# Hymba block on one core: the token division of keys and values moves to 272, and the weights of six kinds start at a different even column in every quarter

## The chip, the cores and the metric

The kernel runs on one core of a Trainium2 chip. The metric is the device time of one execution in microseconds. The engines are named as in the profile: PE multiplies matrices (PEld is its loading of stationary weights), DVE is VectorE, ACT ScalarE, POOL GpSimd, and SP issues most of the DMA transfers.

## The reference

512 tokens and 16 meta tokens in front of them, 528 in all, each 2048 wide, go through one layer. Everything that the change touches belongs to the input projection `P`:

```python
hn = _rmsnorm(h_res, norm_in_g[l])
P = hn @ w_in[l]                    # (528, 2048) @ (2048, 8320)
Pr, Pc = P[..., :RW_COLS], P[..., RW_COLS:]
prev = jnp.pad(Pr[:, :-1], ((0, 0), (1, 0), (0, 0)))
Pr = Pr + (prev - Pr) * mu_shift[l]
...
y = _rwkv7_recurrence(r, decay, k, v, kk, kk * a)   # over the tokens, one after the other
...
y_b = Bg * _causal_depthwise_conv(Cg * hc, conv_w[l]) * jax.nn.silu(g_c)
...
h_res = h_res + jnp.concatenate([y_a, y_b], axis=-1) @ w_out[l]
return _rmsnorm(h_res, norm_f_g)[:, N_META:]
```

The 8320 columns of `w_in` are 65 tiles of 128: eight each of r, k, v, g (group A), one of the two low-rank inputs (lora), and eight each of B, C, h, gc (group B).

## The kernel before

**The input projection.** The input is held transposed, 16 tiles of 128 channels by 528 tokens, as a rounded part `xh` and a remainder `xl`, each of shape 128 x 16 x 576 (576 is `LX`, the room for a channel tile, of which 528 columns are used). A weight tile of 128 output columns over all 2048 channels comes in four quarters of 128 x 512, each holding the stationary weights of four channel tiles. `split_w` (line 135) makes of each quarter a rounded part `hi` on ACT (line 138) and a remainder `lo` on DVE or POOL (line 139). Each product of the projection is three matmuls: hi with xh, hi with xl, lo with xh (line 326). All of them add up in PSUM over the 16 channel tiles.

**The token ranges.** [...] `FULL` serves k, v and lora, which need all 528 tokens; `TAIL` serves r, g, C and h, which need 514; `REAL` serves B and gc, which need 512 and are done in one piece:

```python
FULL = ((0, 256), (256, L))       # L = 528
TAIL = ((14, 272), (272, L))
REAL = ((META, L),)               # META = 16
```

For each quarter, `steps` (line 317) runs the first range over four channel tiles (twelve matmuls) and then the second range over the same four. A tile of k thus has 96 matmuls: 48 of 256 columns and 48 of 272. A tile of r has 48 of 258 and 48 of 256; a tile of B 48 of 512. Each range has its own PSUM tile, which `scaled` copies out on DVE, one operation for each range. `shift_full` and `shift_real` then mix each token with the one before it.

**The weight slots.** `hi` and `lo` lie in one slot of a pool of six, 1088 columns wide, and `parts_of` (line 128) puts them behind an offset of `SHIFT[kind]` columns:

```python
SHIFT = {"lora": 16, "k": 16, "v": 16, "r": 32, "C": 64, "h": 32, "B": 16, "g": 32, "gc": 16, "out": 40}
```

The slots are 1088 columns apart, a multiple of 64, and the rows of xh are 576 apart, also a multiple of 64. So for one kind and one range, every weight block and every moving block start at the same column modulo 64. `kind_of` gives the kind of a stream position.

**The order.** PE's order is written out by hand. `mains` goes through the list `plan`: lora, k, r, B of index 0 first, interleaved quarter by quarter while the input arrives (its first products stand on line 485), and then one tile after the other. Between these matmuls, `fill` puts the smaller products of the recurrence when a given amount of projection work has passed; a matmul of n columns counts 0.43 n ns there. `prefetch` requests weights from SP and splits them two or three half tiles ahead. DVE, ACT and POOL are ordered by a scheduler. After the projection, the output projection runs (lines 1236 and 1445), whose moving weights lie in the same slots with offset 40.

Of the kernel before, what the change touches and what calls it, by code (L numbers as in the profile page):

```python
# [23 lines left out]
L = SEQ + META  # L24
# [50 lines left out]


LX = 576
SHIFT = {"lora": 16, "k": 16, "v": 16, "r": 32, "C": 64, "h": 32, "B": 16, "g": 32, "gc": 16, "out": 40}


@with_exitstack
def hymba_kernel(ctx: ExitStack, tc: tile.TileContext, xt, xtok, front, w_in, w_out, pv, lup, cst, msk, gf, out):
# [27 lines left out]
    plan = [("lora", 0), ("k", 0), ("r", 0), ("B", 0), ("v", 0), ("k", 1), ("r", 1), ("v", 1), ("g", 0), ("g", 1)]  # L110
# [10 lines left out]
    N_IN = len(stream)  # L121
# [5 lines left out]

    def parts_of(kind, name):
        t = wp.tile([P, 2 * 512 + 64], F32R, tag="hl", name=name, bufs=6)
        o = SHIFT[kind]  # L130
        return t[:, o : o + 512], t[:, o + 512 : o + 1024]

    def kind_of(j):
        return "out" if j >= N_IN else plan[j % 4 if j < 8 else j // 2][0]

    def split_w(q, rq, eng):
        hi, lo = parts_of(kind_of(q // 2), f"w{q}")
        nc.scalar.copy(hi, rq)  # L138
        low[q] = eng.tensor_tensor(out=lo, in0=rq, in1=hi.bitcast(F32), op=ALU.subtract).ins  # L139
        quarters[q] = (hi, lo)  # L140
# [36 lines left out]
    def tm(name):  # L177
        return tp.tile([P, LP], F32, tag="tm", name=name, bufs=3)
# [52 lines left out]
    for n in range(4):  # L231
        quarters[2 * n] = parts_of(kind_of(n), f"w{2 * n}")
    F0, F1, F2 = KT + P + L, 4 * P + L, 8 * P + 2 * L
    fr = [view("bt", F0), view("r0", 3 * P), view("bk", F1), view("gt0", F2)]
    o = 0
# [61 lines left out]
    with tc.issue_after(head):  # L297
        nc.vector.tensor_scalar(
            out=omm, in0=pvt[:, V_MU : V_MU + 33], scalar1=-1.0, scalar2=1.0, op0=ALU.mult, op1=ALU.add
        )  # L300
        for d, off in (
# [4 lines left out]
                out=d, in0=pvt[:, off : off + 8], scalar1=0.5, scalar2=None, op0=ALU.mult  # L306
            )
        nc.vector.tensor_scalar(
            out=hv[:, 4], in0=pvt[:, V_KA : V_KA + 8], scalar1=-0.5, scalar2=1.0, op0=ALU.mult, op1=ALU.add
        )  # L310

    nc.scalar.copy(ones, cs[:, C_BM : C_BM + P + 2])
    FULL = ((0, 256), (256, L))
    TAIL = ((14, 272), (272, L))
    REAL = ((META, L),)

# [14 lines left out]
    def banks(ranges, name, pool, tag):  # L331
        return [pool.tile([P, b - a], F32, tag=tag, name=f"ps_{name}_{r}") for r, (a, b) in enumerate(ranges)]

    def main(j, ranges, name):
        prefetch(2 * j + 4)
        ps = banks(ranges, name, pm, "main")
        for k4 in range(4):
            if k4 == 1:
                prefetch(2 * j + 5)
            yield from steps(ps, ranges, k4, 4 * j + k4)  # L340
        return ps

    def scaled(ranges, ps, dst, base):
        for (a, b), p in zip(ranges, ps):
            nc.vector.tensor_tensor(out=dst[:, a - base : b - base], in0=p, in1=rs[:, a:b], op=ALU.mult)

    def shift_full(ps, m, name, dst):
        pr = tp.tile([P, L + 1], F32, tag="pr", name=f"pr_{name}", bufs=2)
        nc.gpsimd.memset(pr[:, 0:1], 0.0)
        scaled(FULL, ps, pr, -1)  # L350
        sh = tm(f"sh_{name}")[:, 0:L]
# [121 lines left out]
    def mains():  # L473
        pa = banks(FULL, "lora", pm, "main")
        pb = banks(FULL, "k0", pz, "tz")
        pc = banks(TAIL, "r0", pm, "main")
        pd = [pi.tile([P, SEQ], F32, tag="ser", name="ps_B0")]
        four = ((pa, FULL), (pb, FULL), (pc, TAIL), (pd, REAL))
        for k in range(4):
            for n, (ps, rg) in enumerate(four):  # L480
                if k == n == 0:
                    hi, lo = quarters[0]
                    for ww, xx, first in ((hi, xh, True), (lo, xh, False), (hi, xl, False)):
                        for p, (a, b) in zip(ps, rg):
                            nc.tensor.matmul(p, ww[:, 0:P], xx[:, 0, a:b], start=first, stop=False)
                            yield (b - a) * 0.43
                    continue
                yield from steps(ps, rg, 0, 2 * n, (k,))
        for k4 in range(1, 4):
            for n, (ps, rg) in enumerate(four):  # L490
                h = 4 * (k4 // 2) + n
                if k4 == 2:
                    prefetch(h + 3)
                if (k4, n) == (3, 3):
                    for ks, part in ((range(1), 0), (range(1, 3), 4), (range(3, 4), None)):
                        yield from steps(ps, rg, k4, 2 * h + k4 % 2, ks)
                        if part is not None:
                            token_scale(yb, part)
                        if part == 4:
                            use("lora", 0, pa)  # L500
                            use("k", 0, pb)
                    continue
                for r in range(2 if n < 3 else 1):
                    if (k4, n, r) == (3, 1, 1):
                        yb = token_scale_sums()
                    yield from steps(ps, rg, k4, 2 * h + k4 % 2, range(4), (r,))
        use("r", 0, pc)
        use("B", 0, pd)
        for j in range(4, len(plan)):
            what, i = plan[j]  # L510
            rg = FULL if what in ("k", "v") else REAL if what in ("B", "gc") else TAIL
            ps = yield from main(j, rg, f"{what}{i}")
            if (what, i) == ("h", 0):
                state["conv"] = low[4 * j + 6]
            if what == "gc" and i < 4:
                state["split"] = low[4 * j + 4]
            use(what, i, ps)
# [646 lines left out]
    U = {unit: u for u, unit in enumerate(units)}  # L1164
# [34 lines left out]
    def split_unit(unit, t, home=None):  # L1199
        for q in range(2):  # L1200
            rq = t()[:, q * 512 : (q + 1) * 512]
            if home is None:
                hi, lo = parts_of("out", f"o{U[unit]}_{q}")
            else:
                hi, lo = home[q]
            nc.scalar.copy(hi, rq)
            last = nc.vector.tensor_tensor(out=lo, in0=rq, in1=hi.bitcast(F32), op=ALU.subtract)  # L1207
            right[unit, q] = (hi, lo)
        if unit[:2] == (1, "M3"):
            last_low[unit[2]] = last.ins  # L1210

    def here(t, n):
        return xa[t][:, n * 512 : (n + 1) * 512] if n < 2 else xb[n - 2][:, t]
# [83 lines left out]
    def split_home(g):  # L1297
        f = ("S1", "S3", "S4", "S5")[g]
        tiles = [
            pw.tile([P, 4, HT], F32R, tag=f"{f}0{a}", name=f"home{g}{a}").rearrange("p a b -> p (a b)") for a in range(2)  # L1300
        ]
        split_unit(
            (1, "M2", g), passing(1, 1, 0, g),
            [(tiles[0][:, 512 * q : 512 * q + 512], tiles[1][:, 512 * q : 512 * q + 512]) for q in range(2)],
        )
# [7 lines left out]
    for half in range(2):  # L1313
        o = 28 * half
        for g in range(4):
            b = o + 4 + 4 * g
            if half == 0:
                if g == 3:
                    at(-1, begin_chain, 0, g)
                    at(0, split_unit, (0, "M1", g), chained(g))  # L1320
            else:
                at(o + g - 4, begin_chain, 1, g)
                at(o + g - 2, split_unit, (1, "M1", g), chained(g))
            at(max(o + g, b - 5), add_by_transfer, half, 0, 1, g)
            at(b - (6 if g else 5), request, half, 0, 1, g)
            at(b - (4 if g else 5), request, half, 1, 1, g)
            at(b - 2, split_unit, (half, "P5", g), chained(g))
            at(b - 1, add, passing(half, 0, 1, g), half, 1, 1, g)
            at(b - 1, split_unit, (half, "M7", g), passing(half, 0, 1, g))
            at(b, split_unit, (half, "M3", g), passing(half, 1, 1, g))  # L1330
            at(b, add, chained(g), half, 1, 1, g)
            at(b + 1, split_unit, (half, "Q6", g), chained(g))
            at(b + 2, add_by_transfer, half, 1, 0, g)
            at(U[half, "P4", g] - 2, split_unit, (half, "P4", g), chained(g))
            if half == 0:
                at(U[half, "M2", g] - 4, request, 0, 1, 0, g)
                at(U[half, "M2", g] - 2, split_unit, (0, "M2", g), passing(0, 1, 0, g))
            else:
                at(o + 13 + 2 * g, request, 1, 1, 0, g)
# [28 lines left out]
    for u, unit in enumerate(units):  # L1368
        half, prod, g = unit
# [53 lines left out]
    with tc.manual_schedule(engines={mybir.EngineType.DVE, mybir.EngineType.Activation, mybir.EngineType.Pool}):  # L1423
# [16 lines left out]
        for part in range(2):  # L1440
            cols = slice(256 * part, 256 * part + 256)
            for jj in range(8):
                hi, lo = right[(1, "M2", jj // 2), jj % 2]
# [4 lines left out]
            h = here(1, 2)[:, cols]  # L1448
# [70 lines left out]
```

## Time and profile before

| what | value |
|---|---|
| median of the runs | 1004.92 us (2 runs, 1004.75 and 1005.09) |
| span of the profiled execution, first to last instruction | 1003.4 us |
| busy time of PE, DVE, ACT, POOL | 992.7, 681.1, 394.9, 272.1 us |
| granted TensorE clock, mean | 0.998 |
| traffic with HBM | 136.92 MB read, 36.35 MB written |

No time of the profiled execution is given beside its span; the median of the runs is 1.5 us longer than that span. In the lists, a matmul or load is a group `line engine op out<-in` with shapes, count, busy time and the mean time of one record. `128*128 128x256` is a stationary block of 128 x 128 and a moving one of 256 columns. Matmuls overlap, so a record is longer than the distance from one start to the next. The chain that ended last gives the pieces of work in order of time, with start, length and count.

### The profile page before, as it was taken

The page shows a single profiled execution, that of the slowest core. Times are in us where ns is not written, and L with a number is a line of the kernel's source. Part 1 is how long each engine was busy: PE and PEld are TensorE (multiplying, and loading weights), DVE is VectorE, ACT ScalarE, POOL GpSimd, SP SyncE. Part 2 cuts the span into 40 slices and gives each one's busy share as a digit, 9 for nine tenths or more (in the row PEclk, how much of TensorE's full clock was granted, in tenths as well). Part 3 has the DMA queues.
Part 4 walks back from the last instruction along what each step waited for, and adds up shares of the span by engine and source line. Part 5 has one row for each costly group of instructions (what it writes and reads, how often), then busy time and mean ns, then how long its engine had stood idle before and what let it go on. Part 6 is the DMA issues. An engine that isn't in the chain of part 4 may idle for free.

```text
span 1003.4 us, 23673 instructions
## 1 busy us (share of the span) xinstructions
PE 992.7 (99%) x9723; PEld 914.6 (91%) x9723; DVE 681.1 (68%) x1247; ACT 394.9 (39%) x729; POOL 272.1 (27%) x284
## 2 busy tenths in 40 slices
PE   9999999999999999999999999999999999999996
PEld 8999999999998999998999998989889898788885
DVE  6777866587765569655569654245554597997897
ACT  7553423344323434323434322223232435546453
POOL 0122524233232323232423223223332333001001
PEclk9999999999999999999999999999999999999999
DMA  9525485546665364864263855968674688797654
GB/s 322 153 90 148 122 222 147 163 122 148 162 167 170 102 166 94 221 163 119 85 171 98 219 148 162 324 204 247 201 228 93 178 267 211 187 299 191 159 127 168
DMA packets 185036, 174.82 MB, mean 174 GB/s; under 512 B 121568, under 2 KB 142816, under 8 KB 184416
## 3 DMA queue, kind: packets, MB, share of 16 engines
q1 hardware_dynamic: 182336, 164.40, 57.0%
q0 software_dynamic: 2304, 8.39, 4.9%
q8 instruction: 76, 1.25, 0.5%
q10 hardware_dynamic: 288, 0.52, 0.1%
q14 instruction: 32, 0.26, 0.1%
HBM read 136.92 MB, written 36.35 MB: 173 GB/s over the span
## 4 chain that ended last, share of the span: by engine, by line
PE 91%; DVE 5%; issue 1%; DMA 1%; ACT 0%; POOL 0%; DVEq 0%; SPq 0%; ACTq 0%; POOLq 0%
PE ps_h L326 9%; PE ps_k L326 9%; PE ps_v L326 9%; PE ps_g L326 9%; PE ps_C L326 9%; PE ps_r L326 9%; PE ps_B L326 9%; PE ps_gc L326 9%; PE M L1236 5%; PE P L1236 2%; PE g L674 2%; DVE o L1207 2%; PE Q L1236 1%; PE ps_lora L326 1%; PE zs L999 1%
## 5 line engine op out<-in xcount | busy, mean ns | idle before, releaser
L139 POOL TENSOR_TENSOR w<-wr,w 128x512 fp32r<-128x512 f32 x119 | 172.2, 1447 | 360.9 <-ACT w L138 305.1
L138 ACT CAST w<-wr 128x512 fp32r<-128x512 f32 x252 | 153.2, 618 | 289.0 <-PE ps_C L326 48.7
L139 DVE TENSOR_TENSOR w<-wr,w 128x512 fp32r<-128x512 f32 x133 | 98.5, 746 | 104.4 <-ACT w L138 104.0
L326 PE MATMUL ps_k<-xh,w 128*128 128x256 f32 (+1 forms) x512 | 96.1, 285 | 0.0
L326 PE MATMUL ps_r<-xh,w 128*128 128x258 f32 (+1 forms) x512 | 95.1, 281 | 0.0
L326 PE MATMUL ps_v<-xh,w 128*128 128x272 f32 (+1 forms) x512 | 94.9, 284 | 0.0
L326 PE MATMUL ps_h<-xh,w 128*128 128x256 f32 (+1 forms) x512 | 94.6, 283 | 0.0
L326 PE MATMUL ps_C<-xh,w 128*128 128x256 f32 (+1 forms) x512 | 93.2, 281 | 0.0
L326 PE MATMUL ps_g<-xh,w 128*128 128x256 f32 (+1 forms) x512 | 92.1, 281 | 0.0
L326 PE MATMUL ps_B<-xh,w 128*128 128x512 f32 x256 | 83.5, 395 | 0.0
L326 PE MATMUL ps_gc<-xh,w 128*128 128x512 f32 x256 | 81.6, 393 | 0.0
L326 PEld LDWEIGHTS ps_k<-xh,w 128*128 128x128 f32 x512 | 80.4, 190 | 0.5
L326 PEld LDWEIGHTS ps_h<-xh,w 128*128 128x128 f32 x512 | 79.6, 188 | 1.3 <-issue 0.6
L326 PEld LDWEIGHTS ps_r<-xh,w 128*128 128x128 f32 x512 | 80.1, 188 | 0.3
L326 PEld LDWEIGHTS ps_v<-xh,w 128*128 128x128 f32 x512 | 79.9, 189 | 0.3
L326 PEld LDWEIGHTS ps_C<-xh,w 128*128 128x128 f32 x512 | 79.2, 188 | 0.6
L326 PEld LDWEIGHTS ps_g<-xh,w 128*128 128x128 f32 x512 | 79.1, 189 | 0.3
L326 PE MATMUL ps_k<-xl,w 128*128 128x256 f32 (+1 forms) x256 | 72.8, 284 | 0.0
L326 PE MATMUL ps_v<-xl,w 128*128 128x256 f32 (+1 forms) x256 | 72.6, 284 | 0.0
L326 PE MATMUL ps_h<-xl,w 128*128 128x258 f32 (+1 forms) x256 | 71.9, 281 | 0.5 <-issue 0.5
L326 PE MATMUL ps_g<-xl,w 128*128 128x258 f32 (+1 forms) x256 | 72.3, 282 | 0.0
L326 PE MATMUL ps_r<-xl,w 128*128 128x258 f32 (+1 forms) x256 | 72.0, 281 | 0.0
(321 smaller groups left out, 2258.9 us busy)
## 6 DMA issues: line engine op xcount, KB each, us to landing
wr<-in_w_in_dram SPq DMA_DIRECT2D x126, 512.0 KB
ct<-opd SPq DMA_DIRECT2D x64, 288.0 KB
wo<-in_w_out_dram SPq DMA_DIRECT2D x24, 512.0 KB
x<-in_w_out_dram POOLq DMA_DIRECT2D x16, 512.0 KB, 6.0
opd<-ar SPq DMA_DIRECT2D x8, 576.0 KB
opd<-gt SPq DMA_DIRECT2D x16, 288.0 KB
opd<-bt SPq DMA_DIRECT2D x64, 64.0 KB
x<-in_w_out_dram SPq DMA_DIRECT2D x8, 512.0 KB
```

What stands on the lines that cost most here:

```text
L138: nc.scalar.copy(hi, rq)
L139: low[q] = eng.tensor_tensor(out=lo, in0=rq, in1=hi.bitcast(F32), op=ALU.subtract).ins
L326: nc.tensor.matmul(ps[r], ww[:, w], xx[:, kt, a:b], start=(kt == 0 and n == 0), stop=(kt == KT - 1 and n == 2))
L674: nc.tensor.matmul(z[h][:, c - c0], bk[hs, c, h : h + 2, :].rearrange("p a s -> p (a s)"), ar[hs, c].rearrange("p a s -> p (a s)"), start= ...
L999: nc.tensor.matmul(d[hs, j], w, x[hs], start=(a == 0), stop=(a == b - 1))
L1207: last = nc.vector.tensor_tensor(out=lo, in0=rq, in1=hi.bitcast(F32), op=ALU.subtract)
L1236: nc.tensor.matmul(bank[s], left(prod, jj, m, s), w, start=(jj == 0 and n == 0), stop=(jj == 7 and n == 2))
```

## The change

Keys, values and lora are divided at token 272 in place of 256, so their two ranges have 272 and 256 columns in place of 256 and 272. The offset of a quarter in its slot depends on the kind, the tile's index `i` and the quarter's number `part` (0 to 3): for k, r and h it is 8 i + 2 part, for v, g and C 62 minus that. Over the eight tiles of a kind, each even number from 0 to 62 occurs once. lora, B and gc keep 16 and the output projection keeps 40.

```diff
-SHIFT = {"lora": 16, "k": 16, "v": 16, "r": 32, "C": 64, "h": 32, "B": 16, "g": 32, "gc": 16, "out": 40}
+OUT_SHIFT = 40
+
+
+def shift_of(what, i, part):
+    if what == "out":
+        return OUT_SHIFT
+    if what in ("B", "gc", "lora"):
+        return 16
+    n = 8 * i + 2 * part
+    return n if what in ("k", "r", "h") else 62 - n
...
     def parts_of(kind, name):
         t = wp.tile([P, 2 * 512 + 64], F32R, tag="hl", name=name, bufs=6)
-        o = SHIFT[kind]
+        o = shift_of(*kind)
         return t[:, o : o + 512], t[:, o + 512 : o + 1024]
...
     def kind_of(j):
-        return "out" if j >= N_IN else plan[j % 4 if j < 8 else j // 2][0]
+        if j >= N_IN:
+            return "out", 0, 0
+        return plan[j % 4] + (j // 4 * 2,) if j < 8 else plan[j // 2] + (j % 2 * 2,)
 
     def split_w(q, rq, eng):
-        hi, lo = parts_of(kind_of(q // 2), f"w{q}")
+        what, i, half = kind_of(q // 2)
+        hi, lo = parts_of((what, i, half + q % 2), f"w{q}")
...
-    FULL = ((0, 256), (256, L))
+    FULL = ((0, 272), (272, L))
```

More of the change, by code (lines that the diff above doesn't have):

```diff
@@ L1202, in split_unit @@
             if home is None:
-                hi, lo = parts_of("out", f"o{U[unit]}_{q}")
+                hi, lo = parts_of(("out", 0, 0), f"o{U[unit]}_{q}")
             else:
```

## The prediction

> **What bounds the kernel now.** I read the page's first two parts, then the waits of PE, then the chain that ended last.
>
> ```profile
> span 1003.4 us, 23673 instructions
> ...
> PE 992.7 (99%) x9723; PEld 914.6 (91%) x9723; DVE 681.1 (68%) x1247; ACT 394.9 (39%) x729; POOL 272.1 (27%) x284
> ...
> PEclk9999999999999999999999999999999999999999
> ```
>
> ```profile
> PE pwarm L187 <- DVE cold L184: 1.4, 1, 1.4
> PE ps_h L326 <- issue: 0.5, 1, 0.5
> PE M L1236 <- DVE o L1207: 0.5, 1, 0.5
> PE ps_lora L326 <- DVE xl L208: 0.2, 1, 0.2
> ```
>
> PE is busy for 99% of the span at a full granted clock, and its four waits sum to 2.6 us. So the time is the sum of the distances between PE's products, and an edit counts only as far as it changes such a distance. The runs' median, 1004.92 us, lies 1.5 us above the span of 1003.4; I carry these 1.5 us along.
>
> The chain shows whole output tiles of the input projection that no other work interrupts (start, length, count of products).
>
> ```profile
> 154.81 10.90 PE ps_gc L326 x48
> ...
> 282.54 11.31 PE ps_h L326 x96
> ...
> 421.11 11.20 PE ps_C L326 x96
> ...
> 469.87 11.57 PE ps_k L326 x96
> ...
> 532.78 11.54 PE ps_v L326 x96
> ...
> 619.32 11.38 PE ps_C L326 x96
> ```
>
> A gc tile is one range of 512 columns: 10.90/48 = 227.1 ns a product, 0.4435 ns a column. The other kinds take two narrow products where gc takes one. At gc's rate a pair of 272 and 256 columns would take 528 x 0.4435 = 234.2 ns; k takes 11.57/48 = 241.0 and v 240.4, so 6.5 ns more. A pair of 258 and 256 would take 228.0; C takes 233.3, later 237.1, and h 235.6: 5.3, 9.1 and 7.6 more, 7.3 in the mean. These excesses are what an address can change. The two C rows have the same widths and the same start columns, so addresses alone do not fix the distance: what stood before on PE matters too.
>
> The timeline shows both shares of a pair. Only every third product reads xl, so two of its rows span three products (start, length).
>
> ```profile
> 421.43 0.28 PE L326 MATMUL ps_C<-xl,w 128*128 128x258 f32 x1
> ...
> 421.79 0.28 PE L326 MATMUL ps_C<-xl,w 128*128 128x258 f32 x1
> ...
> 422.84 0.28 PE L326 MATMUL ps_C<-xl,w 128*128 128x256 f32 x1
> ...
> 423.18 0.28 PE L326 MATMUL ps_C<-xl,w 128*128 128x256 f32 x1
> ```
>
> ```profile
> 471.62 0.29 PE L326 MATMUL ps_k<-xl,w 128*128 128x272 f32 x1
> ...
> 471.99 0.28 PE L326 MATMUL ps_k<-xl,w 128*128 128x272 f32 x1
> ```
>
> So C's 258 columns take 0.36/3 = 120 ns and its 256 take 113, which is gc's rate; k's 272 take 123, which leaves 118 of k's 241 to its 256. The groups by shape say the same over the whole run; the second number behind the bar is the mean record, and of it I use differences alone, since a record also holds a constant tail.
>
> ```profile
> L326 PE MATMUL ps_k<-xh,w 128*128 128x272 f32 x256 | 53.4, 287 | 0.0
> ...
> L326 PE MATMUL ps_C<-xh,w 128*128 128x258 f32 x256 | 52.2, 284 | 0.0
> ...
> L326 PE MATMUL ps_h<-xh,w 128*128 128x256 f32 x256 | 51.7, 282 | 0.0
> L326 PE MATMUL ps_k<-xh,w 128*128 128x256 f32 x256 | 51.6, 283 | 0.0
> L326 PE MATMUL ps_r<-xh,w 128*128 128x256 f32 x256 | 51.1, 279 | 0.0
> L326 PE MATMUL ps_v<-xh,w 128*128 128x256 f32 x256 | 50.6, 281 | 0.0
> ...
> L326 PE MATMUL ps_g<-xh,w 128*128 128x256 f32 x256 | 49.9, 279 | 0.0
> L326 PE MATMUL ps_C<-xh,w 128*128 128x256 f32 x256 | 49.7, 278 | 0.0
> ...
> L1445 PE MATMUL end<-home,m 128*128 128x256 f32 x48 | 5.9, 283 | 0.0
> ...
> L1445 PEld LDWEIGHTS end<-home,m 128*128 128x128 f32 x48 | 5.9, 192 | 0.1
> ```
>
> ```profile
> L326 PEld LDWEIGHTS ps_k<-xh,w 128*128 128x128 f32 x512 | 80.4, 190 | 0.5
> ...
> L326 PEld LDWEIGHTS ps_h<-xh,w 128*128 128x128 f32 x512 | 79.6, 188 | 1.3 <-issue 0.6
> ...
> L326 PEld LDWEIGHTS ps_C<-xh,w 128*128 128x128 f32 x512 | 79.2, 188 | 0.6
> ```
>
> One width, 256, has means from 278 to 283: a band of 5 ns. Of the weight loads (PEld, the second fence), those of L1445 and of k, both with products of 283, are the longest, 192 and 190 ns; C's are 188.
>
> **The change, part by part.** It adds and removes no product, load, copy or transfer. There are 48 tiles of the six kinds with 96 narrow products each, 4608, and lora adds 96. Every count below is of these.
>
> *Division at 272.* The second range of k, v and lora becomes tokens 272 to 527, the moving columns that r, g, C and h have as their second range already, so a row of before shows this product. The means are 283 and 281 for k and v, and 279, 278, 279 and 282 for r, C, g and h: 282.0 against 279.5. If only the moving start counted, this gave 2.5 ns x (16 x 48 + 48 = 816) = 2.0 us. The range of 272 columns now begins at column 0 in place of 256; both are multiples of 64, and I put it at nothing.
>
> *Start columns of the weights.* Before, all offsets of these kinds are 16, 32 or 64, multiples of 16 columns. Afterwards each kind goes once through every even offset from 0 to 62 in its 32 quarters: 28 of 32 are no multiple of 16, and 16 of 32 no multiple of 4. No row of the input projection shows such a start. The bounds from the nearest rows:
> - Below: nothing streams faster than gc's columns. If every excess went, FULL pairs would give 6.5 x 816 = 5.3 us and TAIL pairs 7.3 x 32 x 48 = 11.2 us, in all 16.5.
> - Above: every product at the dear end of the band. The TAIL kinds' 256 go from 279.5 to 283, 3.5 x 1536 = 5.4 us; FULL's from 282 to 283, 0.8 us; the 1536 of 258 and the 816 of 272 columns have no dearer row, so I let them lose the whole band, 5 x 2352 = 11.8 us. In all +18.0.
>
> I take the middle of the band, 280.5, for products that are thrown over all starts: the row nearest to an unknown mixture is neither C's nor L1445's. That is +1.0 x 1536 = +1.5 us for the TAIL kinds' 256, and 280.5 - 282 = -1.5 x 816 = -1.2 us for FULL's, which already holds what is left of the 2.0 us above. For 258 and 272 I take +2 of the possible 5, +4.7 us, because they stand above gc's rate already (120 against 114, 123 against 121) and so may be partly in the bad state now. Sum of both edits: +5.0 us.
>
> [...]
>
> *The start.* lora's first range needs 272 columns of xh in place of 256, and xh's first tile is written in two halves of 264.
>
> ```profile
> 4.04 0.92 ACT L207 ACTIVATE xh<-in_bt 128x264 fp32r<-128x264 f32 x2
> ...
> 4.61 1.50 PE L485 MATMUL ps_lora<-xh,w 128*128 128x256 f32 x4
> ...
> 9.22 0.39 PE L326 MATMUL ps_lora<-xl,w 128*128 128x256 f32 x1 [0.23 <-DVE xl L208]
> ```
>
> PE's first product now waits for the second half, 4.96 in place of some 4.5 us: at most 0.4 us later. Half of this is covered by the 0.23 us that PE waits at 9.22 for VectorE's xl, which comes no later. I add 0.2 us; without cover it is 0.4.
>
> *Splits and evacuations.* The copies and subtractions write to other columns.
>
> ```profile
> L139 POOL TENSOR_TENSOR w<-wr,w 128x512 fp32r<-128x512 f32 x119 | 172.2, 1447 | 360.9 <-ACT w L138 305.1
> L138 ACT CAST w<-wr 128x512 fp32r<-128x512 f32 x252 | 153.2, 618 | 289.0 <-PE ps_C L326 48.7
> ```
>
> ACT waits for PE to free slots (48.7 us behind C alone), so the splits run ahead. A quarter lasts PE about 11.2/4 = 2.8 us, the six slots hold over 16 us, and a split is 0.62 + 1.45 us. Even a doubled POOL part would be hidden; without this cover it would be 1.45 us x 119. The evacuations keep their number. Some DMA issues on SP and a few DVE, ACT and POOL steps change places with a neighbour, behind the same cover. I put all this at nothing.
>
> **Sum:** 1003.4 + 5.0 + 0.2 + 1.5 = 1010.1 us.
>
> **The rivals.**
> *No effect of the weights' start* (0.22). Loads are hidden under products, and only the division counts: 1003.4 - 2.0 + 0.2 + 1.5 = 1003.1, with 1000 to 1005 about it. For it: the C tile at equal addresses differs by 11.38 - 11.20 = 0.18 us, as much as kinds with different offsets do. Against: k, with offset 16, has load records of 190 ns and dear 256s, C 188 and cheap ones.
> [...]
>
> *The varied starts break up the dear state* (0.17). A pair of C went from 233.3 to 237.1 ns and stayed there for a whole tile. If a constant start keeps such a state alive, changing it every quarter would end it. The floor is 1003.4 - 16.5 + 1.5 = 988.4; half of it is 997.
>
> *The load becomes the limit* (0.15), the slower side. Under 113 to 123 ns of product a load has little room: the dearest 256s, k's and L1445's, have the longest ones (against it: h, with 282 ns and loads of 188). If starts off the multiples of 16 lengthen a load by some ns, each narrow product grows by the same, while gc and B hide it under 227. At 5 ns, the band's width, on all 4608 this is 23.0 us: 1003.4 + 23.0 + 1.5 = 1027.9. It passes 2% (20.1 us) from 4.4 ns on all, or 8.7 ns on the half that are no multiples of 4.
>
> That the change does nothing to the program is excluded by the offsets in the diff.
>
> **How the numbers follow.** The forecast, 1006 to 1021, has 0.46. The likeliest time is 1010. The range 994 to 1027 leaves out the lower part of the second rival (0.07) and the upper part of the third (0.10). A change under 2% is about what a measurement of this kernel cannot tell for sure: 2% below is 984.8, under every floor above, so 0.01; 2% above is 1025, reached by most of the third rival, 0.12; between, 0.87.
>
> **What would show it.** In the groups by shape, k's and v's 256 should fall from 283 and 281 to about 280 or 281, those of r, g and C rise by about 1 ns, and 258 and 272 by about 2. In the chain, whole tiles of C above 11.2 us and of k near 11.6. B and gc must keep 10.90. If the means of all narrow shapes stand, the first rival is right; if PEld's records grow by as much as the products, the third. The prediction is wrong if PE gets waits beyond 2.6 us, or if B's and gc's products change.

## The result, and the profile after

The changed kernel takes 1010.9 us (median of 2 runs, 1010.77 to 1011.04) against 1004.92: a ratio of 1.0056, with a 95% interval of 1.004 to 1.0073. Its profiled execution has a span of 1008.8 us, 5.4 more than before.

From the page (the PE and clock rows) and from the list of PE's waits (who waited for whom, sum, times, longest):

```profile
span 1008.8 us, 23672 instructions
...
PE 998.1 (99%) x9723; PEld 919.3 (91%) x9723; DVE 675.7 (67%) x1247; ACT 394.1 (39%) x729; POOL 264.6 (26%) x284
...
PEclk9999999999999999999999999999999999999999
```

```profile
PE pwarm L200 <- DVE cold L197: 1.4, 1, 1.4
PE M L1249 <- DVE o L1220: 0.5, 1, 0.5
PE ps_h L339 <- issue: 0.4, 1, 0.4
PE ps_lora L339 <- DVE xl L221: 0.2, 1, 0.2
```

PE's busy time grew by 5.4 us, as the span did. Its waits sum to 2.5 us (2.6 before), and no DMA or split has moved onto the path. So the loss lies in the distances between products. The chain shows it tile by tile (start, length, count):

```profile
132.46 11.44 PE ps_C L339 x96
143.91 11.42 PE ps_h L339 x96
155.32 10.93 PE ps_gc L339 x48
...
385.67 11.64 PE ps_v L339 x96
...
472.97 11.71 PE ps_k L339 x96
...
802.36 11.38 PE ps_C L339 x96
```

C's first tile went from 11.20 to 11.44 us, h from 11.31 to 11.42, k from 11.57 to 11.71, v from 11.54 to 11.64; the late C tile stands at 11.38, and gc within 0.03. The groups by shape tell which half of a pair it was (mean record behind the second comma):

```profile
L339 PE MATMUL ps_k<-xh,w 128*128 128x272 f32 x256 | 54.2, 288 | 0.0
...
L339 PE MATMUL ps_h<-xh,w 128*128 128x256 f32 x256 | 52.9, 285 | 0.4 <-issue 0.4
L339 PE MATMUL ps_C<-xh,w 128*128 128x258 f32 x256 | 52.1, 284 | 0.0
...
L339 PE MATMUL ps_r<-xh,w 128*128 128x256 f32 x256 | 51.5, 281 | 0.0
...
L339 PE MATMUL ps_k<-xh,w 128*128 128x256 f32 x256 | 51.3, 281 | 0.0
L339 PE MATMUL ps_g<-xh,w 128*128 128x256 f32 x256 | 51.1, 281 | 0.0
L339 PE MATMUL ps_v<-xh,w 128*128 128x256 f32 x256 | 51.0, 280 | 0.0
L339 PE MATMUL ps_C<-xh,w 128*128 128x256 f32 x256 | 50.9, 282 | 0.0
```

The 256 of r, g, C and h rose by 2 to 4 ns, the 272 of k by 1, the 258 of C not at all. Summed over every distance from one start to the next in the two traces, the 5.4 us are: 256 of r, g, C, h +4.3; their 258 -0.9; 272 of k and v +2.0; 256 of k and v -0.2; lora and all the rest +0.3 (the parts are rounded).

### The profile page after: what moved, and what is told of

It reads as the page before. It is cut to its first block, busy times and chain, and to the rows that moved or that the text cites. A ratio compares the mean times of both kernels' runs of the same rounds, so it can differ in the third digit from the quotient of the medians.

```text
span 1008.8 us, 23672 instructions
## 1 busy us (share of the span) xinstructions
PE 998.1 (99%) x9723; PEld 919.3 (91%) x9723; DVE 675.7 (67%) x1247; ACT 394.1 (39%) x729; POOL 264.6 (26%) x284
## 4 chain that ended last, share of the span: by engine, by line
PE 93%; DVE 3%; DMA 1%; issue 1%; ACT 0%; SPq 0%; DVEq 0%; POOL 0%; ACTq 0%
PE ps_v L339 9%; PE ps_k L339 9%; PE ps_h L339 9%; PE ps_g L339 9%; PE ps_r L339 9%; PE ps_B L339 9%; PE ps_gc L339 9%; PE ps_C L339 8%; PE M L1249 5%; PE P L1249 4%; PE g L687 2%; PE Q L1249 2%; DVE o L1220 1%; PE ps_lora L339 1%; PE zs L1012 1%; PE zy L1016 1%
## 5 line engine op out<-in xcount | busy, mean ns | idle before, releaser
L152 POOL TENSOR_TENSOR w<-wr,w 128x512 fp32r<-128x512 f32 x119 | 164.4, 1383 | 381.7 <-ACT w L151 330.9
L152 DVE TENSOR_TENSOR w<-wr,w 128x512 fp32r<-128x512 f32 x133 | 95.4, 723 | 114.0 <-ACT w L151 103.8
L339 PE MATMUL ps_k<-xh,w 128*128 128x272 f32 (+1 forms) x512 | 96.5, 285 | 0.0
L339 PE MATMUL ps_v<-xh,w 128*128 128x256 f32 (+1 forms) x512 | 96.4, 285 | 0.0
L339 PE MATMUL ps_k<-xl,w 128*128 128x272 f32 (+1 forms) x256 | 73.0, 285 | 0.0
L339 PE MATMUL ps_v<-xl,w 128*128 128x272 f32 (+1 forms) x256 | 72.8, 284 | 0.0
```

What stands on the lines that cost most here:

```text
L339: nc.tensor.matmul(ps[r], ww[:, w], xx[:, kt, a:b], start=(kt == 0 and n == 0), stop=(kt == KT - 1 and n == 2))
```

## The experiments

Each kernel is the kernel before with the edit shown. Ratios are to runs of the kernel before on the same chip, with their 95% interval. "Distance" below is the start column of a product's weights in their slot less the start column of its tokens in the row of xh, modulo 64. The two areas are taken to begin at the same place modulo 64 columns. The traces do not show this; if it were otherwise, every distance would be off by one constant, and no comparison below would change.

### The two edits alone

```diff
-    FULL = ((0, 256), (256, L))
+    FULL = ((0, 272), (272, L))
```

> Only the division of keys, values and lora at token 272; all offsets of the weights as before. If the moving start decides, as the prediction took it, the 256 columns of k and v fall by about 2.5 ns each and the 272 stand: 2.0 us less than before, 1002.9. Rival: at offset 16 the 272 keep their 123.5 ns and the 256 go to about 119.4, which is what the few quarters with offset 16 show in the changed kernel; then it is 1.4 us more than before, 1006.3. If the division alone were the cause of the whole loss it would be 1010.9.

1007.17 us, ratio 1.0021 (1.0012 to 1.003). The second edit alone is the diff of the change with `FULL` left at 256.

> Only the changing offsets of k, v, r, g, C and h; division at 256 as before. If the loss lies in the weights' starts: 4 to 6 us more than before, 1009 to 1011, with the 256-column products of r, g, C and h some 2.5 ns dearer and their 258 unchanged, as in the changed kernel. If the two edits need each other: 1005, as before.

1010.03 us, ratio 1.0049 (1.0036 to 1.0061). Both edits cost time. 2.1 and 5.0 are more than the 6.0 of the pair, but the intervals leave room for a plain sum. In the traces the 256 of k and v do not add: +1.1 us with the division alone, +0.8 with the starts alone, -0.2 with both. The groups by shape of the division alone:

```profile
L326 PE MATMUL ps_k<-xh,w 128*128 128x272 f32 x256 | 54.0, 289 | 0.0
L326 PE MATMUL ps_v<-xh,w 128*128 128x272 f32 x256 | 53.7, 289 | 0.0
...
L326 PE MATMUL ps_k<-xh,w 128*128 128x256 f32 x256 | 52.0, 284 | 0.0
...
L326 PE MATMUL ps_v<-xh,w 128*128 128x256 f32 x256 | 51.6, 282 | 0.0
```

The 256 did not fall to 279.5: with 284 and 282 they are 1 ns dearer than before (283, 281), though they now move the very columns that r's do. Their weights' start differs from r's, and so does the range before them (272 columns at 0, for r 258 at 14). That rules out the moving start as the sole cause.

### The start itself, or the change from quarter to quarter

```diff
-    n = 8 * i + 2 * part
-    return n if what in ("k", "r", "h") else 62 - n
+    n = 16 * part
+    return n if what in ("k", "r", "h") else 48 - n
```

(In `shift_of` of the change, with the division at 256.)

> Division at 256; the offset changes in every quarter, but among 0, 16, 32 and 48 alone (16 times the quarter's number for k, r, h, 48 minus that for v, g, C). Theory of the start (starts that are no multiples of 16 columns are dear): nothing changes against before, 1005, and C keeps its 113.3 ns for 256 columns. Theory of the change (a constant start lets PE settle in a cheap state, and each new start throws it out): 1008 to 1011, with C's 256 near 118.

1008.96 us, ratio 1.004 (1.0027 to 1.0054). In the other kernel the three returned lines are one table, `{"k": 20, "v": 20, "r": 36, "g": 36, "h": 36, "C": 4}[what]`, again with the division at 256.

> Division at 256; the offset is constant for a kind, as before, but 4 columns off a multiple of 16 for all six kinds (k and v 20, r, g and h 36, C 4). Theory of the start: dearer than before by as much as the changed kernel, 1008 to 1011, and C's 256 no longer at 113.3. Theory of the change: 1005, with a settled cheap state in C and h.

1012.28 us, ratio 1.0072 (1.0059 to 1.0084). Each theory is refuted by one of the two kernels: multiples of 16 can be dear, and a constant start can be dearer than a changing one. The timeline of one h tile of the first of these kernels shows why. Its four quarters have the offsets 0, 16, 32 and 48; of each quarter's 256-column products the first and the last that read xl are shown, nine products apart, so that 0.01 us in these rows is 1 ns a product (start, length):

```profile
284.62 0.28 PE L339 MATMUL ps_h<-xl,w 128*128 128x256 f32 x1
...
285.68 0.28 PE L339 MATMUL ps_h<-xl,w 128*128 128x256 f32 x1
...
287.46 0.28 PE L339 MATMUL ps_h<-xl,w 128*128 128x256 f32 x1
...
288.55 0.28 PE L339 MATMUL ps_h<-xl,w 128*128 128x256 f32 x1
...
290.35 0.28 PE L339 MATMUL ps_h<-xl,w 128*128 128x256 f32 x1
...
291.37 0.28 PE L339 MATMUL ps_h<-xl,w 128*128 128x256 f32 x1
...
293.13 0.28 PE L339 MATMUL ps_h<-xl,w 128*128 128x256 f32 x1
...
294.19 0.28 PE L339 MATMUL ps_h<-xl,w 128*128 128x256 f32 x1
```

1.06/9 = 118 ns at offset 0, 1.09/9 = 121 at 16, 1.02/9 = 113 at 32, 1.06/9 = 118 at 48. The tokens of this range start at column 272, that is 16 modulo 64, so the cheap quarter is the one at a distance of 16, the dear one that at 0. This made the third theory, that the distance has the price. The runs so far bear it out for the 256 columns: their tokens start at column 0 (k, v, division at 256) or 16 modulo 64 (r, g, C, h, and k, v with the division at 272), and the mean time from start to start, sorted by column distance, is much the same for the two (mean over the quarters of the kernels before and after the change and of the four above, times over 170 ns left out):

```
column distance    tokens at 0     tokens at 16
0                  119.0 ns        119.5 ns
2                  116.2           116.2
4                  118.5           118.2
16                 117.2           115.6
20                 118.9           118.8
22                 115.2           115.5
32                 119.3           118.7
40                 119.8           119.9
44                 118.2           118.1
48                 117.8           116.3
```

Ten of the 32 even distances are shown. On the left those at 2, 4, 22, 40 and 44 rest on one or two quarters each (at 22 a second one, with other work between its products, had 117.0). Over all 32 distances the two columns differ by 0.7 ns (root mean square) and by 1.7 at most. Sorted by the weights' offset alone, without the tokens' start, they would differ by 1.6 and 3.6. So the distance orders these times, and the offset does not.

The two largest differences in the table, at 16 and 48, have another reason: at these distances nearly every quarter lies at one of two levels. At 16, 151 of 234 quarters with tokens at 16 average 114 to 116 ns and 72 average 118; with tokens at 0 it is 14 of 83 and 66. At 48 with tokens at 16, 34 of 106 average 113 and 63 average 118. At 0 and 20 there is no low level: all quarters average 117 to 120. So in these six kernels the levels go with the distance, and something else chooses between them.

### The distance, tested directly

Tokens and weights are moved together by 4 columns, which leaves every distance as it was:

```diff
-    xh = xp.tile([P, KT, LX], F32R, name="xh")
-    xl = xp.tile([P, KT, LX], F32R, name="xl")
+    xh = xp.tile([P, KT, LX], F32R, name="xh")[:, :, 4 : 4 + L]
+    xl = xp.tile([P, KT, LX], F32R, name="xl")[:, :, 4 : 4 + L]
...
-SHIFT = {"lora": 16, "k": 16, "v": 16, "r": 32, "C": 64, "h": 32, "B": 16, "g": 32, "gc": 16, "out": 40}
+SHIFT = {"lora": 20, "k": 20, "v": 20, "r": 36, "C": 4, "h": 36, "B": 20, "g": 36, "gc": 20, "out": 40}
```

> Division at 256. Every weight offset of the input projection is 4 columns larger (lora, k, v, B, gc 20, r, g, h 36, C 4, which is 68 less 64), and the tokens in xh and xl start 4 columns later too. Theory of the distance (what counts is the start of the weights less the start of the moving columns, modulo 64 columns): all distances are those of the kernel before, so 1005, with k's 256 near 117 ns and its 272 at 123.5. Theory of the start (a weights' start off the multiples of 16 is dear by itself): 1012, as with the constant offsets that were 4 larger and the tokens left in place, 256 of r, g and h at 118.8.

1002.64 us, ratio 0.9977 (0.9968 to 0.9986). The same weight offsets that cost 7.2 us with the tokens in place now gain 2.2. So these offsets are not dear by themselves: what they cost depends on where the tokens start. But the distance is not all, since equal distances should have given 1005. Before, B's group was

```profile
L326 PE MATMUL ps_B<-xh,w 128*128 128x512 f32 x256 | 83.5, 395 | 0.0
```

and with 4 columns on both sides

```profile
L326 PE MATMUL ps_B<-xh,w 128*128 128x512 f32 x256 | 84.4, 398 | 0.0
...
L326 PE MATMUL ps_k<-xh,w 128*128 128x256 f32 x256 | 50.1, 277 | 0.0
```

k's 256 fell from 283 to 277, B's 512 rose from 395 to 398. For k and v it is the level that changed: before, 51 of their 64 quarters of 256 columns averaged 118 ns and 2 averaged 113 or 114, here it is 1 and 45. Two more shifts, by 8 and by 2 columns on both sides, and one that puts B's and gc's weights back:

> Division at 256; weights of the input projection and tokens both start 8 columns later (lora, k, v, B, gc 24, r, g, h 40, C 8), so all distances are those of the kernel before. Theory of the distance alone: 1005, every shape within half a ns of before. With 4 columns on both sides the narrow products became 1 to 3 ns cheaper and the 512 of B and gc 4 ns dearer, so the place itself has a price too. If that price belongs to starts that are odd multiples of 4 columns, 8 gives 1005 again, with 512 at 227.8; if it grows with the shift, 512 go above 232.

1005.4 us, ratio 1.0002 (0.9993 to 1.0012): k's 256 at 282, B's 512 at 395, as before. Not every shape stayed within half a ns: C's 256 rose from 115.3 to 116.7 ns, mainly because its first two tiles in the chain are now in the dear level and only the next two in the cheap one, with the same start columns:

```profile
132.00 11.38 PE ps_C L326 x96
...
271.22 11.38 PE ps_C L326 x96
...
421.29 11.20 PE ps_C L326 x96
...
570.88 11.20 PE ps_C L326 x96
```

The run by 2 columns:

> The same with 2 columns (lora, k, v, B, gc 18, r, g, h 34, C 2). Theory of the distance alone: 1005. If starts off the multiples of 8 columns make the 512 dearer and the narrow ones cheaper, as with 4: 512 above 230, k's and v's 256 below 116, 1002 to 1006.

1017.6 us, ratio 1.0121 (1.0107 to 1.0136): the dearest of all. The 512 did go above 230 (231.6 ns from start to start), but the 256 of k and v, expected below 116, take 119.8. This expectation missed. No quarter of the six kinds has a cheap level there: their 256 average 119 to 121 ns in every quarter, at distances that had 113 to 118 before.

> As with 4 columns on both sides, but B and gc keep the offset 16, so that their weights stand 60 columns from their tokens, modulo 64, in place of 0. If the 512 became dearer by their weights' start: they fall from 232 to 227.8 and the kernel to 1002.6 - 3.2 = 999.4. If by their tokens' start: they stay at 232 and the time at 1002.6.

1002.56 us, ratio 0.9971 (0.9959 to 0.9982). The 512 keep 231.8 ns from start to start (232.0 with offset 20, 227.8 before). So it is the tokens' start that makes them dear. In all: with equal distances a shift by 8 columns leaves the time as it was (1005.4 us), by 2 or 4 it does not (1017.6 and 1002.64). For the 512 the place of the tokens has a price beside the distance: 3.8 to 4.2 ns at shifts by 2 and 4 columns, none at 8. For the narrow products tokens and weights were moved together, so whose place counts there is not separated.

### Division at 272 with the distance mended

```diff
-SHIFT = {"lora": 16, "k": 16, "v": 16, "r": 32, "C": 64, "h": 32, "B": 16, "g": 32, "gc": 16, "out": 40}
+SHIFT = {"lora": 32, "k": 32, "v": 32, "r": 32, "C": 64, "h": 32, "B": 16, "g": 32, "gc": 16, "out": 40}
...
-    FULL = ((0, 256), (256, L))
+    FULL = ((0, 272), (272, L))
```

> Division at 272, and k, v and lora at offset 32 in place of 16; nothing else. Theory of the distance: the 256 of k and v now stand 16 columns from their weights, as those of r, g and h do, and fall from 119.5 (division alone) to 115 or 116 ns; the 272 go from a distance of 16 to 32 and rise from 124 to 126.5. Sum against the division alone: (-4 + 2.5) x 816 = -1.2 us, 1006. Theory of the moving start, as the prediction had it: the 256 were cheap at any offset; then this is as the division alone, 1007, with the 256 at 119.5.

1004.68 us, ratio 0.9998 (0.9988 to 1.0007), 2.5 us below the division alone.

```profile
L326 PE MATMUL ps_k<-xh,w 128*128 128x272 f32 x256 | 54.6, 290 | 0.0
L326 PE MATMUL ps_v<-xh,w 128*128 128x272 f32 x256 | 54.6, 291 | 0.0
...
L326 PE MATMUL ps_k<-xh,w 128*128 128x256 f32 x256 | 49.7, 277 | 0.0
...
L326 PE MATMUL ps_v<-xh,w 128*128 128x256 f32 x256 | 49.5, 277 | 0.0
```

Between the division alone and this kernel only the weights' offset of k, v and lora differs, and the same 256 columns go from 284 and 282 to 277, the 272 from 289 to 290 and 291. From start to start the 256 went from 119.5 to 114.0 ns and the 272 from 124.2 to 126.6. Both go the way that the distance says, and the 272 by the amount expected; the 256 fell further than the 115 or 116 expected, because almost all of their quarters are now in the cheap level.

### Which constant starts are cheap

r, g, h and C at one offset; k and v stay at 16, the division at 256. First 54, then 64:

> Division at 256; r, g, C and h all at the constant offset 54, k and v at 16. In the changed kernel the quarters with offset 54 had 116.8 ns for 256 columns and 117.6 for 258, 234.4 for the pair, against 236 in the mean before. Theory of the distance: the price belongs to the offset, so every pair falls to 234.4: 1.6 x 1536 = 2.5 us less than before, 1002.5. Theory of the change (a constant start lets PE settle): also 1005 or less. If 54 was cheap only by what stood before it: 1005 or more.

> Division at 256; r, g, h at offset 64 like C. C had two states at this offset: 233.3 ns a pair in its first four tiles, 237.1 in the last four. If the state is carried on from one tile to the next, r, g, C and h settle in one of the two together: 1001 if the cheap one (2.7 x 1536 less), 1006.5 if the dear one. If the offset alone had a price, the pairs would take the mean of C's, 235.2, and it would be 1004.

54 gives 1001.95 us, ratio 0.9971 (0.996 to 0.9982); 64 gives 1006.69, ratio 1.0019 (1.001 to 1.0028). The chain of the kernel with 54:

```profile
131.58 11.20 PE ps_C L326 x96
142.78 11.20 PE ps_h L326 x96
...
617.06 11.20 PE ps_C L326 x96
```

Every uninterrupted tile of C and h in the chain has 11.20, the late C among them. It is not the cheap level of before: the 256 of r, g, C and h became dearer by 2.1 us in all (C's from 115.3 to 116.9 ns) and their 258 cheaper by 4.6 us (C's from 119.7 to 117.0). So the gain lies in the 258, whose distance is now 40. The chain of the kernel with 64:

```profile
132.19 11.39 PE ps_C L326 x96
143.57 11.39 PE ps_h L326 x96
...
571.70 11.39 PE ps_C L326 x96
```

Here C's first four tiles, whose offset is what it was before, went from 11.20 to 11.39, while only r, g and h in front of them were moved. So with C's start columns equal PE has two states, 11.20 and 11.38 or 11.39 us a tile, and what ran before helps to choose. Each is kept through an uninterrupted tile: in the kernel before, the 256 of C's tiles at 132.30 and 421.11 us take 113.9 to 114.2 ns in all four quarters, those at 619.32 and 797.07 take 117.6 in all four. That one tile hands its state to the next would fit, but it is not shown: in the kernel with 8 columns on both sides C's first two tiles are dear and the next two cheap. What puts PE into the one or the other stays open.

Last, k and v at 22 on top of 54:

> The version with r, g, C and h at 54 (1001.95), and k and v at 22 in place of 16; division at 256. In the run with the changing offsets alone, quarters at 22 had 115.2 ns for k's and v's 256 columns and 124.3 for their 272: 239.5 a pair, against 240.7 at 16. Theory of the distance: 1.2 x 768 = 0.9 us less than with 54 alone, 1001.0. If that was chance in the one quarter of 256 columns that stood there undisturbed: 1002.

1001.5 us, ratio 0.9965 (0.9952 to 0.9979), the fastest version; its k tile:

```profile
467.73 11.43 PE ps_k L326 x96
```

11.43 us in place of 11.57. Against 54 alone, which ran on another chip, the median is 0.45 us lower, and the intervals overlap, so the gain in the whole time is not settled. The tile gained 0.14 us where 1.2 x 48 ns = 0.06 were expected: the direction is what the distance said, the size is not.

## Why the prediction was right in its sum and wrong in its parts

**What bounds the kernel** was right: PE's busy time carries the change, its waits stay at 2.5 us, B and gc keep their 10.90 us within 0.04.

The sum came out by luck: the 256 of r, g, C and h cost 2.8 us more than forecast, those of k and v 1.0 and the 272 0.4 more, and the 258 4.0 less.

**Division at 272.** The step that failed is "the second range of k, v and lora becomes the moving columns that r, g, C and h have as their second range already, so a row of before shows this product". It took the moving start for the cause. The price goes with the distance: r's weights stand 16 columns from these tokens, k's with offset 16 stand at 0 (115.6 and 119.5 ns in the table). The rows of before could not show this, since the 256 of k, v, r, g and h all stand at a distance of 16 there. What set the 283 and 281 of k and v apart from r's 279 was mainly the level: 51 of 64 quarters of k and v average 118 ns, 61 of 96 of r, g and h 114 to 116. (k's 283 also holds four records of 384 to 415 ns; without them it is 281.) In place of -2.0 us the division alone costs 2.1. "The range of 272 columns now begins at column 0 ... I put it at nothing" held for the distance, but in the run with the division alone the 272 rose from 287 to 289 (0.6 ns from start to start).

**Start columns of the weights.** The bounds held, and +5.0 for both edits came close to 5.4. Its parts did not: I put +1.5 us on the 256 of r, g, C and h, which took 4.3; -1.2 on the 256 of k and v, which took -0.2; and +4.7 on the 258 and 272, of which the 272 took 2.0 where 816 x 2 = 1.6 were forecast, while the 258 gained 0.9 where 1536 x 2 = 3.1 were to be lost. "Middle of the band" was mis-sized: r, g and h had 115.7 ns before, near the cheap end of all distances, and of the other even ones most cost 117 to 120; afterwards the same three have 118.3. The band itself was read from records, with the words "a record also holds a constant tail". The tail is not constant: by their records the 256 of k and v went from 283 and 281 to 281 and 280, from start to start from 117.7 and 116.9 to 117.9 and 118.0 ns, so the gain in the list was none in time. For the 258 the prediction's own remark that they "stand above gc's rate already" spoke for a smaller loss than the +2 ns it put there; they gained 0.6 ns.

**The start of the kernel.** The first product came at 5.05 us in place of 4.61, and the wait for xl in the next tile stayed 0.23 us. In neither kernel is the first product part of the chain that ended last: that goes from a later piece of the input, which landed at 7.61 us before and at 7.27 now, over its xh and xl to lora's products at 9.22 and 8.89. So the +0.2 us had no part in the sum. The later start was also made up on the way: before, the seven products after the first follow at 213 to 226 ns, now at 181 and then 116 to 125. No run shows why.

**The rivals.** *No effect of the weights' start* fell with the run of the starts alone (1010.03 us, ratio 1.0049). The products of 256 columns of k and v also went from 284 and 282 to 277 ns between the division alone and the division with offset 32, where nothing but the start of weights moved. So the time of these narrow products does depend on where their weights lie. *The varied starts break up the dear state* fell too: C's early tiles were in the cheap state, 11.20 us, and lost it, with 11.39 to 11.44. *The load becomes the limit* fell by its own test, that the records of the loads grow with the products. The loads of the changed kernel (mean behind the second comma):

```profile
L339 PEld LDWEIGHTS ps_h<-xh,w 128*128 128x128 f32 x512 | 79.7, 188 | 1.3 <-issue 0.6
L339 PEld LDWEIGHTS ps_k<-xh,w 128*128 128x128 f32 x512 | 80.4, 188 | 0.4
...
L339 PEld LDWEIGHTS ps_C<-xh,w 128*128 128x128 f32 x512 | 79.6, 188 | 0.6
```

k's loads went from 190 to 188 while its 272 became dearer. In the dearest kernel, with 2 columns on both sides, C's loads have 190, 2 ns more than before, while its 256 rose by 4.6; so the two are not without a link, but the loads do not grow by as much as the products. Whether an offset is a multiple of four columns, as half of them are, did not decide: offsets that are all multiples of four columns gave the dearer 1012.28 us. In the changed kernel and the one with the starts alone, quarters at multiples of four columns and the others, with 16 offsets each, average 118.3 and 118.1 ns for 256 columns, 119.7 and 119.8 for 258, 125.6 and 125.4 for 272.

## What to carry to other kernels

Where PE is busy throughout, read the distance from start to start of single shapes, by tile: here products of 256 columns took 113 to 121 ns by quarter, and this kernel moved between 1001.5 and 1017.6 us by start columns alone, with the division at 256. Change one operand's start at a time, and then both by the same amount: that tells a price of a place from a price of a distance. A row of before prices a changed product only if both operands start where they will start, and then only if its tiles all have one level: here r's 279 ns did not price k's 256, which took 284, and C's 256 had 113.9 or 117.6 ns with equal starts. Take the price from the starts: the recorded lengths of k's 256 fell by 2 ns, from 283 to 281, while the distance from start to start went from 117.7 to 117.9.

## What the hardware showed

With these rounded 32-bit products, the time from start to start depends on the start of the weights less the start of the moving columns (256 columns: from 115 to 120 ns in the table), although both are read from different tiles. It is taken modulo 64 columns here, as the tiles are laid out; no run tries another period. It depends on the place of the moving columns as well: 512 columns take 227.8 ns when shifted by 0 or 8 columns (mean record of B 395 in both) and 231.6 to 232.0 by 2 or 4; no run tries another shift. At some distances there are two states with equal start columns (256 columns at 48: 113 or 118 ns; 11.20 and 11.39 us a tile of C), each kept through an uninterrupted tile. Neither why the distance counts nor what chooses the state was shown by any run.
